# A transformer layer in split fp32 on one core: weight sums moved to VectorE, more warming products, softmax scaling issued a slot later, output weights rounded earlier, norm loads two steps ahead

## The chip, the cores and the metric

The kernel runs on one core of a Trainium2 chip. A core has five engines that work side by side, each through its own queue in order: TensorE (PE, matrix products, with a loader PEld for the stationary operand), VectorE (DVE), ScalarE (ACT), GpSimd (POOL) and SyncE (SP, which here only issues transfers). 16 DMA engines move data between HBM and the on-chip memory. Products accumulate in PSUM banks; the other operands lie in SBUF. The metric is the device time of one execution in microseconds (us); less is better. Engines wait for one another through semaphores.

## What is computed

One layer of a streaming encoder on x of 2048 tokens by 1024, all in float32:

```python
h = rms_norm(x, g_pre_mix[i])
m = chunk_relpos_attention(h, w_qkv[i], w_o[i], rel_bias[...])
x = x + rms_norm(m, g_post_mix[i])
h = rms_norm(x, g_pre_ffn[i])
x = x + rms_norm(swiglu(h, w_gate[i], w_up[i], w_down[i]), g_post_ffn[i])

def chunk_relpos_attention(h, w_qkv, w_o, rel_bias):
    q, k, v = split_heads(h, w_qkv)               # 16 heads of 64
    for c in range(n_chunks):                     # chunks of 64 frames
        ...                                       # keys: the chunk and the 8 before it
        sc = einsum('bhqd,bhkd->bhqk', q_blk, k[:, :, k0:k1]) * scale + bias
        p = softmax(sc)
        outs.append(einsum('bhqk,bhkd->bhqd', p, v[:, :, k0:k1]))
    return merge_heads(concatenate(outs)) @ w_o

def swiglu(h, w_gate, w_up, w_down):              # inner width 2816
    return (silu(h @ w_gate) * (h @ w_up)) @ w_down
```

## The kernel before

**Products.** Each float32 operand is split into a rounded high part and the rest: ACT copies it to the fast float32 format (`hi`), DVE subtracts that from the original (`lo`). `split_part` (L131, L132) does it for weights, `split` (L341, L342) for activations. A product is then three matmuls, high by high, high by low and low by high (`products`, L185 to L187), so in the profile each product shows as L185, L186 and L187.

**Seven block products.** The projections (V, then Q and K), gate/up and down are computed in 2 by 2 blocks with seven products and not eight, in the order B11, B21, T1, T2, B22, T3, T4 of activation blocks; each has a weight factor, A11, A12, S1, S2, S4, S3 or A22. S1 to S4 are sums or differences of weight blocks A. The tokens are worked in two groups of 1024 (g = 0, 1). In group 0, `block_items` loads the A blocks, and `sum_` (L834) makes the sums in place, on POOL, and stores each to HBM by a transfer from POOL's queue (L835); in group 1, `stored_items` loads them back. There are 68 sums: 8 for V, 16 for Q/K (4 chunks of columns), 44 for gate/up (11 chunks). A weight goes through a `Stream`, which loads and splits a few items ahead of PE's use; its float32 copies lie in a ring of eight tiles (`w4`, called raw in the profile), the split ones in a ring of four (`w`).

**Stages**, by their place in the span: the projections (`project`, 0 to about 505 us: V of group 0 until about 100, Q/K of group 0 until about 305, then group 1), attention (505 to 1162), the last part of the output product (to 1200), gate/up of group 0 (1200 to 1650), and the rest of the feed-forward network (to the end).

**The start.** PE first does nine products of 128 x 128 on an identity (L1256, two rows each in the profile), then V's first blocks as x arrives. The pre-norm is not applied to x but to the products: the sum of squares goes to `ms` (mean square, on DVE: L275 in the first token half, L1301 where it comes from ACT's squares by token, L1297), POOL raises it to −1/2 (`hr`, L277, L1302), and PE spreads it (`prs`, L337); `add_square` (L252, L253) collects the squares. Q and K are scaled (L420) and split (L422, L423) as they come, after DVE has added up the block products (L1224).

**Attention.** 128 slots, each two heads by 128 queries; 32 slots make a quarter of the tokens. `scores` (of slot t + 3) makes PE's scores (`st`, L493, L494), on DVE the sum with the bias and the row extreme (L502), on ACT the exponential and row sums (L506), on DVE the reciprocal (L510) and on POOL the scaling (L513). `transposed` (of slot t) turns the weights by PE (`tt`, L528; out to `pT` by DVE L531 and ACT L533), `fifth` the last block of keys (L542, L543), and `output` (after four slots) multiplies with v (L558) and splits the result (L341, L342). Between the slots, `fill` works off the output product of the quarter before (`o_quarter`, `mm` in the profile); in the first quarter there is none. `take` fetches its weights a slab ahead (`fetch`: load and split, 32 loads in all).

**Background steps.** Norm sums and residual additions (`Blocks.sums`, `Late.sums`, `Late.write`) are lists of steps, taken from the deque `later` as PE's products are issued (`tick`). `behind(w, n, lag, load, use)` lays a loop out so that the load of step k stands `lag` steps ahead of its use. Their tiles come from small rings (`scratch` of four, `io` of three).

**What sets the order.** PE's order is that of the program. On DVE, ACT, POOL and SP a scheduler sets it from the dependencies and the place in the program, so moving a statement need not move its instruction; each queue then runs in order.

Of the kernel before, what the change touches and what calls it, by code (L numbers as in the profile page):

```python
# [9 lines left out]
F32 = mybir.dt.float32  # L10
F32R = mybir.dt.float32r
I32 = mybir.dt.int32
AF = mybir.ActivationFunctionType
# [36 lines left out]
def trunk(  # L50
# [79 lines left out]
    def split_part(hi, lo, raw):  # L130
        act.activation(hi, raw, AF.Copy)  # L131
        dve.tensor_tensor(lo, raw, hi.bitcast(F32), op=ALU.subtract)  # L132

    def fetch():
        n = len(ready)
        if n == len(plan):
            return
        tiles = [w_tile(f"{n}_{c}") for c in range(2)]
        for c in range(2):
            here = slice(c * 1024, c * 1024 + 1024)  # L140
            if "fp" in phase:
                part = phase["fp"].tile([P, 1024], F32, tag="w4", name=f"raw_{n}_{c}", bufs=phase["w4"])
            else:
                part = phase["ap"].tile([P, 1024], F32, tag="raw", name=f"raw_{n}_{c}", bufs=2)
            sp.dma_start(part, plan[n][:, here])
            split_part(*tiles[c], part)
        ready.append(tiles)

# [17 lines left out]

    def take(ahead=True):

        n = taken[0]
        taken[0] += 1  # L170
        if len(ready) == n:
            fetch()
        if ahead:
            fetch()
        return Slab(ready[n])
# [256 lines left out]
    class Attend:  # L432
# [45 lines left out]
        def scores(self, ib):  # L478
# [17 lines left out]
            for h in range(2):  # L496
# [11 lines left out]
                )  # L508
                self.sc[ib, h] = sc
            dve.reciprocal(rows[:, 2:4], rows[:, 0:2])  # L510
            for h in range(2):
# [33 lines left out]
        def output(self):  # L545
# [16 lines left out]
            if p == 0:  # L562
                ats[n] = Cols(((0, 1), (2, 3))[n % 2])
            split(ats[n].hi(p), ats[n].lo(p), po)

    def o_quarter(n):
# [4 lines left out]
        for d2 in range(KT // 2):  # L571
            w = take()
            if last and d2 == KT // 2 - 1:
                back.ahead(-2)
            for dt in (2 * d2, 2 * d2 + 1):
                pt = dense_bank(dt)
                c = slice((dt % 2) * P, (dt % 2) * P + P)
                for k in range(KT):
                    products(pt, w.hi(k, c), w.lo(k, c), src.hi(k), src.lo(k), k == 0, k == KT - 1)
                    yield 3 * C512  # L580
                t = io("y")
                act.activation(t, pt, AF.Copy)
                sp.dma_start(o_d[n][:, dt, :], t)
                add_square(pt, osums[n], dt == 0)

    class Blocks:
# [8 lines left out]
        def sums(self, w, on_all=False):  # L595
# [4 lines left out]
            for t in range(2):  # L600
# [13 lines left out]

                steps += behind(w, KT, 1, load, use)
                if on_all:
# [206 lines left out]
    def block_items(src, key, early=True, ahead=None):  # L823
# [9 lines left out]
        def sum_(name, to, a, b, op=ALU.add):  # L833
            pool.tensor_tensor(r[to], r[a], r[b], op=op)  # L834
            last_pool[0] = pool.dma_start(sums_d[key][name], r[to])  # L835
# [248 lines left out]
    class Late:  # L1084
# [5 lines left out]
        def sums(self, w):  # L1090
# [10 lines left out]

            return behind(w, KT, 1, load, use)

# [11 lines left out]
        def write(self, w, eng=dve):  # L1115
# [14 lines left out]

            return behind(w, KT, 1, load, use)

# [119 lines left out]
    def project():  # L1252

        warm = ps.tile([P, HALF], F32, tag="mm", name="warm")
        for _ in range(9):
            pe.matmul(warm[:, 0:P], ident, ident, start=True, stop=True)  # L1256
# [268 lines left out]
    for t in range(AHEAD):  # L1525
        ahead(t)
    for t in range(slots):
        share = (0.4 if t % 4 == 0 else 1.2) * left[0] / max(per - t % per - 1, 1)
        if t > 0 and t % 4 == 0:
            fill(0.45 * share)  # L1530
            jobs[t // 4 - 1].output()
            if t % per == 0:
# [13 lines left out]
    jobs[-1].output()  # L1546
    fill(1e9)
# [91 lines left out]
```

## Time and profile before

| | |
|---|---|
| three runs | 2500.98, 2501.5, 2511.96 us; median 2501.5 |
| the profiled execution | 2506.22 us, of it 2504.4 from the first to the last instruction (the span) |
| mean granted clock of TensorE | 0.982 |
| HBM traffic | 529.73 MB moved by DMA, 212 GB/s on average |

The profile tells, for every instruction, its engine, line, tiles (out<-in), start and length, and what ended the idle time before it. "PE prs L337 <- POOL hr L1302" reads: PE was idle ahead of the instruction of line 337 that writes prs, until POOL's instruction of line 1302, which writes hr, was done. x and a number is how many. The granted clock is the share of TensorE's full clock that it ran at. The rows themselves stand in the prediction.

### The profile page before, as it was taken

The page shows a single profiled execution, that of the slowest core. Times are in us where ns is not written, and L with a number is a line of the kernel's source. Part 1 is how long each engine was busy: PE and PEld are TensorE (multiplying, and loading weights), DVE is VectorE, ACT ScalarE, POOL GpSimd, SP SyncE. Part 2 cuts the span into 40 slices and gives each one's busy share as a digit, 9 for nine tenths or more (in the row PEclk, how much of TensorE's full clock was granted, in tenths as well). Part 3 has the DMA queues.
Part 4 walks back from the last instruction along what each step waited for, and adds up shares of the span by engine and source line. Part 5 has one row for each costly group of instructions (what it writes and reads, how often), then busy time and mean ns, then how long its engine had stood idle before and what let it go on. Part 6 is the DMA issues. An engine that isn't in the chain of part 4 may idle for free.

```text
span 2504.4 us, 33018 instructions
## 1 busy us (share of the span) xinstructions
PE 2360.5 (94%) x11442; PEld 1914.6 (76%) x11442; DVE 1672.8 (67%) x2557; ACT 1162.8 (46%) x2039; POOL 498.2 (20%) x490
## 2 busy tenths in 40 slices
PE   7899999978888899898999999999999999999998
PEld 6677788856666677666888878888888888888887
DVE  8768856556555565566977687676657657555567
ACT  6443743346555565565532333355443333334454
POOL 4223012123332433431433233300000000000002
PEclk8999999989999999999999999999999999999999
DMA  6466789999767877784576654457765755547654
GB/s 252 161 228 215 250 240 325 298 240 258 215 169 194 244 201 204 227 230 156 185 249 222 219 180 156 151 202 226 235 237 170 249 182 190 175 146 246 193 188 153
DMA packets 229783, 529.73 MB, mean 212 GB/s; under 512 B 26320, under 2 KB 42720, under 8 KB 225136
## 3 DMA queue, kind: packets, MB, share of 16 engines
q1 hardware_dynamic: 217712, 480.42, 60.9%
q0 software_dynamic: 11904, 47.19, 6.2%
q8 instruction: 91, 1.49, 0.3%
q14 instruction: 76, 0.62, 0.1%
HBM read 380.14 MB, written 170.44 MB: 220 GB/s over the span
## 4 chain that ended last, share of the span: by engine, by line
PE 54%; DVE 2%; ACT 1%; issue 1%; DMA 0%; POOL 0%; DVEq 0%; SPq 0%; ACTq 0%
PE pd L187 6%; PE pd L185 6%; PE pd L186 6%; PE pb L186 4%; PE pb L187 4%; PE pb L185 4%; PE pc L186 3%; PE pc L187 3%; PE pc L185 3%; PE pa L185 3%; PE pa L186 3%; PE pa L187 3%; PE po L558 1%; PE mm L187 1%; PE mm L185 1%; PE mm L186 1%
## 5 line engine op out<-in xcount | busy, mean ns | idle before, releaser
L513 POOL TENSOR_SCALAR sc<-sc,rows 128x640 f32<-128x640 f32 (+4 forms) x256 | 194.7, 773 | 399.7 <-DVE rows L510 197.7
L834 POOL TENSOR_TENSOR raw<-raw,raw 128x1024 f32<-128x1024 f32 x68 | 179.9, 2646 | 394.3 <-DMA raw<-in_w_gu 139.6
L506 ACT ACTIVATE sc<-sc,rows 128x640 f32<-128x640 f32 (+4 forms) x256 | 192.9, 755 | 112.6 <-DVE rows L502 112.4
L502 DVE CUSTOM_DVE_ANT_0 sc<-st,bias 128x640 f32<-128x640 f32 (+2 forms) x248 | 176.0, 746 | 86.0 <-PE st L494 60.4
L185 PE MATMUL pb<-hb,w_wg_T 128*128 128x512 f32 x528 | 205.6, 389 | 0.0
L187 PE MATMUL pb<-hb,w_wg_T 128*128 128x512 f32 x528 | 205.4, 389 | 0.0
L186 PE MATMUL pb<-hb,w_wg_T 128*128 128x512 f32 x528 | 205.4, 389 | 0.0
L528 PE MATMUL tt<-ident,sc 128*128 128x128 f32 x928 | 140.6, 281 | 45.6 <-DVE pT L531 21.5
L277 POOL TENSOR_TENSOR rs<-ms,neg_half 128x4 f32<-128x4 f32 (+1 forms) x7 | 7.9, 1125 | 854.8 <-DVE ms L275 854.8
L528 PEld LDWEIGHTS tt<-ident,sc 128*128 128x128 f32 x928 | 105.0, 143 | 82.2 <-issue 72.1
L493 PE MATMUL st<-k,q 128*128 128x384 f32 (+3 forms) x440 | 140.7, 340 | 28.0 <-DVE rows L502 23.1
L187 PE MATMUL pd<-a,w_d_T 128*128 128x512 f32 (+1 forms) x368 | 139.8, 380 | 0.1
L185 PE MATMUL pa<-hb,w_wg_B 128*128 128x512 f32 x352 | 137.7, 391 | 2.4 <-ACT terms L922 2.4
L185 PE MATMUL pd<-a,w_d_T 128*128 128x512 f32 (+1 forms) x368 | 139.9, 380 | 0.0
L186 PE MATMUL pd<-a,w_d_T 128*128 128x512 f32 (+1 forms) x368 | 139.7, 380 | 0.0
L186 PE MATMUL pa<-hb,w_wg_B 128*128 128x512 f32 x352 | 137.7, 391 | 0.0
L187 PE MATMUL pa<-hb,w_wg_B 128*128 128x512 f32 x352 | 137.5, 391 | 0.0
L943 ACT ACTIVATE terms<-terms 128x512 f32<-128x512 f32 x65 | 41.1, 632 | 195.9 <-DVE terms L941 195.9
L494 PE MATMUL st<-k,q 128*128 128x384 f32 (+3 forms) x440 | 129.9, 315 | 0.0
L531 DVE COPY pT<-tt 128x512 f32<-128x512 f32 (+3 forms) x128 | 81.6, 637 | 69.6 <-ACT hb L341 36.2
L342 DVE TENSOR_TENSOR a<-raw_a,a 128x512 fp32r<-128x512 f32 x154 | 105.7, 694 | 30.1 <-ACT a L341 29.9
L558 PE MATMUL po<-pT,v 128*64 128x384 f32 (+3 forms) x864 | 125.2, 436 | 0.0
(265 smaller groups left out, 6343.6 us busy)
## 6 DMA issues: line engine op xcount, KB each, us to landing
raw<-in_w_gu SPq DMA_DIRECT2D x77, 512.0 KB, 4.1
q<-q SPq DMA_DIRECT2D x62, 512.0 KB, 6.7
k<-k SPq DMA_DIRECT2D x55, 512.0 KB, 9.2
s_g_S<-raw POOLq DMA_DIRECT2D x44, 512.0 KB, 3.1
raw_d<-d_S SPq DMA_DIRECT2D x88, 256.0 KB, 3.6
raw_a<-aT SPq DMA_DIRECT2D x88, 256.0 KB, 3.6
raw<-s_g_S SPq DMA_DIRECT2D x44, 512.0 KB, 3.8
bias<-ext_d SPq DMA_DIRECT2D x124, 144.0 KB, 9.2
```

What stands on the lines that cost most here:

```text
L185: pe.matmul(pt, a_hi, b_hi, start=first, stop=False, skip_group_check=go_on)
L186: pe.matmul(pt, a_hi, b_lo, start=False, stop=False, skip_group_check=go_on)
L187: pe.matmul(pt, a_lo, b_hi, start=False, stop=last, skip_group_check=go_on)
L342: eng.tensor_tensor(lo, src, hi.bitcast(F32), op=ALU.subtract)
L493: pe.matmul(st[:, a:b], q[:, 2 * h, cols], kk[:, h, key], start=True, stop=False)
L494: pe.matmul(st[:, a:b], q[:, 2 * h + 1, cols], kk[:, h, key], start=False, stop=True)
L502: dve.tensor_tensor_reduce(out=sc[:, :n], in0=st[:, c0 : c0 + n], in1=rev, scale=-1.0, scalar=3.0e38, op0=ALU.add, op1=ALU.min, accum_out= ...
L506: act.activation(sc[:, :n], sc[:, :n], AF.Exp, bias=nmax, scale=-1.0, accum_out=rows[:, h : h + 1])
L513: last_pool[0] = pool.tensor_scalar(sc[:, :n], sc[:, :n], rows[:, 2 + h : 3 + h], 1.0, op0=ALU.mult, op1=ALU.mult)
L528: pe.transpose(tt[:, u, :], sc[h][:, b * P : b * P + P], ident)
L558: pe.matmul(po[heads[h], c0:c1], v[:, kb, c : c + 64], self.pT[:, h, r, c0:c1], start=m == 0, stop=m == len(terms) - 1,)
L834: pool.tensor_tensor(r[to], r[a], r[b], op=op)
```

## The change

Five parts:

1. `sum_` adds on DVE and no longer on POOL; the store remains on POOL's queue.
2. 28 warming products, not 9.
3. `scores` ends after the exponentials; the reciprocal and the scaling are a new method `scaled`, called in the next slot, between `transposed` and the new scores. `output` only rounds the high part and returns a function for the low part, which runs after the new scores.
4. Output weights: `fetch` only loads a slab, `part_split` splits half of it, in the middle and near the end of every second output tile of the slab ahead. The first slab is loaded at slot 16 and split at slots 20 and 22.
5. `behind` has lag 2 in `Blocks.sums`, `Late.sums` and `Late.write`.

```diff
+    raws = []
     def fetch():
-        n = len(ready)
+        n = len(raws)
...
             sp.dma_start(part, plan[n][:, here])
-            split_part(*tiles[c], part)
-        ready.append(tiles)
+            parts.append(part)
+        raws.append(parts)
+
+    def part_split(c):
+        n = len(ready) - (c > 0)
+        if n == len(raws):
+            return
+        if c == 0:
+            ready.append([w_tile(f"{n}_{i}") for i in range(2)])
+        split_part(*ready[n][c], raws[n][c])
...
-    def take(ahead=True):
+    def take():
...
+        if len(raws) == n:
+            fetch()
         if len(ready) == n:
-            fetch()
-        if ahead:
-            fetch()
+            part_split(0)
+            part_split(1)
+        fetch()
...
+            self.open = (ib, rows, n)
+
+        def scaled(self):
+            ib, rows, n = self.open
             dve.reciprocal(rows[:, 2:4], rows[:, 0:2])
...
-            split(ats[n].hi(p), ats[n].lo(p), po)
+            act.activation(ats[n].hi(p), po, AF.Copy)
+            return lambda: dve.tensor_tensor(ats[n].lo(p), po, ats[n].hi(p).bitcast(F32), op=ALU.subtract)
...
                     yield 3 * C512
+                    if k == 3 and len(ready) == taken[0] and dt % 2:
+                        part_split(0)
+                    elif k == KT - 2 and dt % 2 and len(ready) > taken[0]:
+                        part_split(1)
...
-                steps += behind(w, KT, 1, load, use)
+                steps += behind(w, KT, 2, load, use)
...
         def sum_(name, to, a, b, op=ALU.add):
-            pool.tensor_tensor(r[to], r[a], r[b], op=op)
+            dve.tensor_tensor(r[to], r[a], r[b], op=op)
             last_pool[0] = pool.dma_start(sums_d[key][name], r[to])
...
-        for _ in range(9):
+        for _ in range(28):
             pe.matmul(warm[:, 0:P], ident, ident, start=True, stop=True)
...
     for t in range(AHEAD):
         ahead(t)
+        if t < AHEAD - 1:
+            jobs[0].scaled()
...
-            jobs[t // 4 - 1].output()
+            low = jobs[t // 4 - 1].output()
...
+        if t == 16:
+            fetch()
+        elif t in (20, 22):
+            part_split(t // 2 - 10)
         job = jobs[t // 4]
         job.transposed(t % 4)
+        if t + AHEAD - 1 < slots:
+            jobs[(t + AHEAD - 1) // 4].scaled()
         ahead(t + AHEAD)
+        if t > 0 and t % 4 == 0:
+            low()
```

How the scheduler lays the queues out, in three places. The new program's line numbers are higher: L253 is L265 there, L342 is L354, L675 is L697, L275 is L287, the sum's L834 is L856, L1297 is L1319, L510 is L527, L502 is L514, L531 is L548.

DVE at the start, before (w_wv are V's weights, hb the blocks of x, total the sum of squares):

```order
10 L132 TENSOR_TENSOR w_wv_B_330<-raw_283,w_wv_B_330 128x1024
11 L132 TENSOR_TENSOR w_wv_B_339<-raw_285,w_wv_B_339 128x1024
12 L253 TENSOR_TENSOR total<-total,sq 128x512 x2
13 L342 TENSOR_TENSOR hb_4_357<-hb_2_287,hb_4_357 128x512 x2
14 L253 TENSOR_TENSOR total<-total,sq 128x512 x2
15 L342 TENSOR_TENSOR hb_4_357<-hb_2_287,hb_4_357 128x512 x2
16 L675 TENSOR_TENSOR hb_1_276<-hb_1_276 128x512
17 L275 TENSOR_SCALAR ms<-pssq 128x4
18 L132 TENSOR_TENSOR w_wv_T_434<-raw_289,w_wv_T_434 128x1024
```

DVE at the same place now (two rows more of total, hb_4 and sums stand ahead of these, like them):

```order
18 L265 TENSOR_TENSOR total<-total,sq 128x512
19 L354 TENSOR_TENSOR hb_4_376<-hb_2_306,hb_4_376 128x512
20 L265 TENSOR_TENSOR total<-total,sq 128x512
21 L856 TENSOR_TENSOR raw_313<-raw_313,raw_315 128x1024
22 L354 TENSOR_TENSOR hb_4_376<-hb_2_306,hb_4_376 128x512
23 L856 TENSOR_TENSOR raw_300<-raw_300,raw_313 128x1024
24 L697 TENSOR_TENSOR hb_1_295<-hb_1_295 128x512
25 L856 TENSOR_TENSOR raw_304<-raw_304,raw_300 128x1024
26 L354 TENSOR_TENSOR hb_5_443<-hb_1_295,hb_5_443 128x512
27 L132 TENSOR_TENSOR w_wv_T_453<-raw_308,w_wv_T_453 128x1024
28 L132 TENSOR_TENSOR w_wv_T_456<-raw_313,w_wv_T_456 128x1024
29 L287 TENSOR_SCALAR ms<-pssq 128x4
```

The root's `ms` stood right behind the subtractions of hb_4 and stands now behind six sums (L856), the first subtraction of hb_5 and two weight roundings; the sums alternate with the subtractions that PE waits for.

ACT, the squares by token (L1297, of `terms` tiles that SP fills) in the V stage, before:

```order
58 L1297 ACTIVATE terms,ssq<-terms 128x1024
59 L341 ACTIVATE hb_6_554<-hb_1_276 128x512
60 L1169 ACTIVATE terms<-pv 128x512
61 L131 ACTIVATE w_wv_B_625<-raw_283 128x1024
62 L131 ACTIVATE w_wv_B_628<-raw_285 128x1024
63 L695 ACTIVATE t_800<-hb_1_276 128x512
64 L1297 ACTIVATE terms,ssq<-terms 128x1024
65 L695 ACTIVATE t_801<-hb_1_276 128x512
66 L695 ACTIVATE t_802<-hb_1_276 128x512
67 L695 ACTIVATE t_803<-hb_1_276 128x512
68 L341 ACTIVATE hb_8_741<-hb_1_276 128x512 x3
69 L1297 ACTIVATE terms,ssq<-terms 128x1024
```

and now:

```order
48 L1319 ACTIVATE terms,ssq<-terms 128x1024
49 L1191 ACTIVATE terms<-pv 128x512
50 L717 ACTIVATE t_819<-hb_1_295 128x512
51 L1191 ACTIVATE terms<-pv 128x512
52 L353 ACTIVATE hb_6_573<-hb_1_295 128x512
53 L717 ACTIVATE t_820<-hb_1_295 128x512
54 L353 ACTIVATE hb_6_573<-hb_1_295 128x512
55 L1319 ACTIVATE terms,ssq<-terms 128x1024
```

The last of the four squarings, which the second root needs, stood ahead of row 70 and stands ahead of row 56; the two weight roundings w_wv_B, which stood ahead of it, stand behind it.

DVE in an attention slot, before and now, where the reciprocal of a slot is written a slot later in the program:

```order
813 L531 COPY pT<-tt 128x4x128 [waits PE_49]
814 L510 RECIPROCAL rows<-rows 128x2 [waits Activation_49]
815 L502 ISA sc,rows<-st,bias_4109 128x640 [waits DMAHW0_49,DMAHW7_49,PE_49,Pool_49]
816 L502 ISA rows 128x1
817 L502 ISA sc,rows<-st,bias_4114 128x640 [waits DMAHW2_49,DMAHW1_49]
```

```order
835 L548 COPY pT<-tt 128x4x128 [waits PE_49]
836 L527 RECIPROCAL rows<-rows 128x2 [waits Activation_49]
837 L514 ISA sc,rows<-st,bias_4125 128x640 [waits DMAHW0_49,DMAHW7_49,PE_49,Pool_49]
838 L514 ISA rows 128x1
839 L514 ISA sc,rows<-st,bias_4130 128x640 [waits DMAHW2_49,DMAHW1_49]
```

The reciprocal stands where it stood, behind the copy of the turned weights and ahead of the next slot's scores, and waits for the same engine; so it is in nearly all slots.

More of the change, by code (lines that the diff above doesn't have):

```diff
@@ L132, in split_part @@
         dve.tensor_tensor(lo, raw, hi.bitcast(F32), op=ALU.subtract)
+    raws = []
     def fetch():
-        n = len(ready)
+        n = len(raws)
         if n == len(plan):
             return
-        tiles = [w_tile(f"{n}_{c}") for c in range(2)]
+        parts = []
         for c in range(2):
@@ L1100, in use @@
                 add_square(c.pop(dt), self.total, dt == 0)
-            return behind(w, KT, 1, load, use)
+            return behind(w, KT, 2, load, use)
         def rstd(self, wait):
@@ L1129, in use @@
                 sp.dma_start(self.dst[:, dt, :], y)
-            return behind(w, KT, 1, load, use)
+            return behind(w, KT, 2, load, use)
     rs, rows_of = [], {}
@@ L1540, in trunk @@
                     later.extend(blocks[0].sums(2.0))
+        if t == 16:
+            fetch()
+        elif t in (20, 22):
+            part_split(t // 2 - 10)
         job = jobs[t // 4]
         job.transposed(t % 4)
+        if t + AHEAD - 1 < slots:
+            jobs[(t + AHEAD - 1) // 4].scaled()
         ahead(t + AHEAD)
+        if t > 0 and t % 4 == 0:
+            low()
         fill((0.55 if t % 4 == 0 else 1.0) * share)
         job.fifth()
-    jobs[-1].output()
+    jobs[-1].output()()
     fill(1e9)
```

## The prediction

> **What bounds the kernel now.** I read the page's totals first, then TensorE's waits, then busy time by stretch, then timelines around each long wait.
>
> ```profile
> PE 2360.5 (94%) x11442; PEld 1914.6 (76%) x11442; DVE 1672.8 (67%) x2557; ACT 1162.8 (46%) x2039; POOL 498.2 (20%) x490
> ...
> PE st L493 <- DVE rows L502: 29.9, 34, 5.2
> PE pb L185 <- DVE terms L1224: 13.1, 5, 4.0
> PE prs L337 <- POOL hr L1302: 9.6, 1, 9.6
> PE mm L185 <- ACT w L131: 6.9, 2, 3.7
> PE tt L528 <- DVE rows L510: 6.3, 6, 1.1
> PE pv L187 <- DVE hb L342: 5.6, 5, 2.3
> ```
>
> TensorE (PE) works 2360.5 of 2504.4 us, so the whole idle time that any edit can win back is 144 us, plus what a cold clock costs. The change adds no product but small warming ones, so it must earn its gain from the waits above (us in total, times, longest).
>
> ```profile
> 0.00:50.00 50.00, 37.45 (x131) 28.56 (x131) 40.02 (x31) 29.36 (x46) 27.26 (x23) 0.83 0.66 262
> 50.00:100.00 50.00, 39.55 (x157) 31.18 (x158) 40.03 (x58) 32.65 (x52) 4.01 (x3) 0.86 0.41 138
> 305.00:495.00 190.00, 190.00 (x840) 157.36 (x839) 115.97 (x153) 77.02 (x105) 34.80 (x48) 1.00 0.94 287
> 1200.00:1250.00 50.00, 50.00 (x225) 41.50 (x224) 46.66 (x51) 28.63 (x45) 21.91 (x13) 1.00 0.50 176
> 1300.00:1650.00 350.00, 344.81 (x1517) 284.42 (x1516) 256.07 (x290) 118.30 (x161) 104.02 (x65) 1.00 0.53 181
> ```
>
> The columns are length, busy time of PE, its loader, VectorE (DVE), ScalarE (ACT) and GpSimd (POOL), granted clock, DMA share. PE idles 12.6 and 10.5 us in the first two stretches and runs at 0.83 and 0.86 of its clock; from 305 to 495 it never idles (840 products in 190 us, 0.226 us each); in the first token group of gate/up (1200 to 1650) it idles next to nothing in the first 50 us and 5.2 in the last 350. So gains are to be had at the start, in the Q/K products behind it and in attention, and hardly in the feed-forward part, where 44 of the 68 moved sums lie.
>
> **Part 1, the sums on DVE.** A sum costs POOL 2646 ns, and it stretches what DVE does beside it.
>
> ```profile
> L834 POOL TENSOR_TENSOR raw<-raw,raw 128x1024 f32<-128x1024 f32 x68 | 179.9, 2646 | 394.3 <-DMA raw<-in_w_gu 139.6 <-DVE w_wg_B L132 91.2 <-DVE w_wq_B L132 53.7
> ...
> 14.69 1.29 DVE L342 TENSOR_TENSOR hb<-hb,hb 128x512 fp32r<-128x512 f32 x2
> 18.44 6.44 DVE L253 TENSOR_TENSOR total<-total,sq 128x512 f32<-128x512 f32 x2
> 24.80 6.65 DVE L342 TENSOR_TENSOR hb<-hb,hb 128x512 fp32r<-128x512 f32 x2
> 34.64 1.22 DVE L132 TENSOR_TENSOR w_wv_T<-raw,w_wv_T 128x1024 fp32r<-128x1024 f32 x1
> 37.80 8.35 DVE L132 TENSOR_TENSOR w_wv_T<-raw,w_wv_T 128x1024 fp32r<-128x1024 f32 x1
> ```
>
> Alone, two half-width (512) operations take 1.29 us, 0.65 each, and a 1024-wide one 1.22; beside POOL's sums the same forms take 6.44, 6.65 and 8.35. In these three rows DVE loses 5.2 + 5.4 + 7.1 = 17.7 us. A sum on DVE isn't in the trace; its bounds are the 1024-wide subtraction (1.22) and POOL's 2.65. I take 1.22, the same engine and shape: 8 sums at the start cost 9.8 us and give back 17.7.
>
> Now the path. PE there waits for two roots of norms, whose rows are these, in order of time:
>
> ```profile
> 34.80 1.96 POOL L277 TENSOR_TENSOR hr<-ms,neg_half 128x4 f32<-128x4 f32 x1 [3.92 <-DVE ms L275]
> 38.23 1.05 PE L337 MATMUL prs<-ident,hr 128*128 128x128 f32 x4
> 50.20 0.64 PE L187 MATMUL pv<-w_wv_T,hb 128*128 128x512 f32 x1 [1.82 <-DVE hb L342]
> 74.09 1.06 ACT L1297 ACTIVATE terms<-terms 128x1024 f32<-128x1024 f32 x1 [1.39 <-DMA terms<-in_xt]
> 75.53 1.04 POOL L1302 TENSOR_TENSOR hr<-ms,neg_half 128x4 f32<-128x4 f32 x1 [25.55 <-DVE ms L1301]
> 76.63 1.11 PE L337 MATMUL prs<-ident,hr 128*128 128x128 f32 x4 [9.63 <-POOL hr L1302]
> ```
>
> *First root.* In the new order ms stands behind 6 sums, 9 half-width operations and 2 weight roundings: from 18.4, that is 8 x 1.22 + 9 x 0.65 = 15.6 us, so ms at 34.0 to 34.3, just ahead of the root as before (34.80). The root, 1.96, ends at 36.3 and prs starts at 36.5 instead of 38.23, where PE still had products to do: −1.7. But PE, whose operands now come without stretch (its waits for hb were up to 2.3 us), is done by about 30 and stands there idle: the waits for hb are replaced by one for the root of some 6 us. *This is what is late next.*
>
> *Second root.* PE's second prs was ready at 67.0 (76.63 less its wait of 9.63), 28.8 us after the first, with 1.82 us of that in the gap before 50.20 and, behind it, some 8 products at half clock (0.2 us each too much, 1.6; the pitch is worked out in part 2). Without these it is ready at 36.5 + 28.8 − 3.4 = 61.9. Its release: ACT squares the tokens in four pieces, the last at 74.09; in the new order these stand some 14 rows earlier, as do their loads. DVE ahead of that ms has 26 half-width rows and 6 wide ones, 16.9 + 7.3 = 24.2 us, from 34.3: not before 58.5. With some 4 us of waits for PE's and ACT's results I take ms at 62.6 and, 1.5 us on, prs at 64.1, against 76.63: **−12.5**. Bounds: −14.7 (PE ready, 61.9), and −2 (the last squaring stays where it was, only the first root's gain is left).
>
> *Q/K.* These rows stand just ahead of the waits for L1224:
>
> ```profile
> 145.88 2.40 DVE L420 TENSOR_TENSOR terms<-terms,row 128x512 f32<-128x512 f32 x1
> 148.97 2.72 DVE L423 SCALAR_TENSOR_TENSOR lo<-terms,hi 128x512 fp32r<-128x512 f32 x1 [0.70 <-ACT hi L422]
> 155.51 0.47 PE L185 MATMUL pb<-hb,w_wq_T 128*128 128x512 f32 x1 [3.99 <-DVE terms L1224]
> 195.22 2.84 DVE L423 SCALAR_TENSOR_TENSOR lo<-terms,hi 128x512 fp32r<-128x512 f32 x1
> 198.70 2.77 DVE L420 TENSOR_TENSOR terms<-terms,row 128x512 f32<-128x512 f32 x1
> 198.81 0.47 PE L185 MATMUL pb<-hb,w_wq_T 128*128 128x512 f32 x1 [2.91 <-DVE terms L1224]
> ```
>
> At 146 to 151, DVE loses 1.75 + 2.1 = 3.8 us by the half-width price, and PE waits 3.99; at 195 to 201 it loses 2.2 + 2.1 = 4.3, and PE waits 2.91 and then again. One or two sums now stand in the same queue, 1.2 to 2.4 us each time. So 1.4 to 3.1 us come back each time, **−4** for both. The rest of the 13.1 us has no sum beside it. Bounds: 0 to −8.1 (no sum in the way).
>
> *Gate/up.* 44 sums add 44 x 1.22 = 54 us to DVE. What comes back:
>
> ```profile
> L952 DVE TENSOR_TENSOR T<-terms,T 128x512 f32<-128x512 f32 x43 | 51.4, 1196 | 0.1
> L952 DVE TENSOR_TENSOR T<-b,terms 128x512 f32<-128x512 f32 x22 | 15.1, 686 | 0.1
> ...
> POOL raw L834 <- DMA raw<-in_w_gu: 139.6, 9, 32.6
> ```
>
> 43 x (1196 − 686) = 22 us in one group; at the start of the program a sum cost DVE more than it will itself, here the other groups were stretched less. DVE's load grows by nothing to 32 us in 450, and what PE waits there, 5.2 us, is all that can be won: **−2**, bounds −5.2 and +14 (second rival). POOL waited nine times for the weights themselves; DVE will now wait there in its place, with the evacuations of PE's banks queued behind it.
>
> **Part 2, warming.** 19 more products add 38 rows to 18. At the row's own 0.234 us they end at 14.4, past the first product:
>
> ```profile
> 1.35 4.21 PE L1256 MATMUL warm<-ident 128*128 128x128 f32 x18 [1.35 <-POOL ident masks.py:199]
> 10.22 0.80 PE L185 MATMUL pv<-w_wv_B,hb 128*128 128x512 f32 x1 [4.66 <-ACT hb L341]
> 18.30 0.63 PE L187 MATMUL pv<-w_wv_B,hb 128*128 128x512 f32 x1
> 18.72 0.63 PE L185 MATMUL pv<-w_wv_B,hb 128*128 128x512 f32 x1
> ```
>
> From start to start a product takes 0.42 us here, and 0.226 at full clock (840 in 190 us, above). If the clock came up only late, this part would cost 14.4 − 10.2 = 4.2 us; if it were up at 10.2, the 8.5 us until 18.72 would shrink by up to a half, 4. Both vanish in PE's new wait of some 6 us for the first root, which they end before: 0, with −4 to +4 only where that wait isn't there. [...]
>
> **Part 3, reciprocals and scaling a slot later.** In DVE's new order the reciprocals stand, in almost every slot, where they stood: the scheduler had put them there already. POOL's scalings and the low halves likewise. I cost it 0; the wait that it is about is 6.3 us on PE, and it could also cost as much.
>
> **Part 4, output weights.**
>
> ```profile
> 630.44 0.61 PE L185 MATMUL mm<-hb,w 128*128 128x512 f32 x1 [3.73 <-ACT w L131]
> 629.35 1.99 ACT L131 ACTIVATE w<-raw 128x1024 fp32r<-128x1024 f32 x2
> ```
>
> At the end of the first quarter PE waits 3.73 us while ACT rounds the first slab (1.99) behind its exponentials, then 9 products run at half clock: 3.7 + 9 x 0.2 = 5.5. The slab is now rounded in the slots 20 and 22, where DVE's rows hold PE up (29.9 us in all) and two subtractions can add at most 2 x 1.22 = 2.4. I take **−4**; bounds −5.5 and +2.4. Later slabs move half a slab, between attention rows of the same number: 0.
>
> **Part 5, norms two steps ahead.** Their tiles come from a ring of four that is full already; SP's loads keep their places. 0, bounds ±3.
>
> **Sum.** −12.5 − 4 − 2 − 4 = −22.5, from the profiled execution's 2506.2 (span 2504.4): 2483.7. That execution stands 4.7 above the median, 2501.5, of the runs shown; measured from there, **2479**.
>
> **Rivals.** *The second root stays late.* ms stands behind DVE's whole queue; if waits in that queue, which now hold also for the loads of the weights, push it to 73, the start gives 2 and not 12.5: −12, 2490. For it: DVE was busy 40 us of each 50 there; against: 17.7 of that was stretch. Chance 0.2, a quarter of it beyond the 0.5% line.
>
> *DVE blocks on weights (slower).* At each of 11 chunks the first sum stands in DVE's queue within some microseconds of its load's landing, POOL waited 139.6 us in nine such places, and DVE works 46.7 of the first 50 us. Where the wait exceeds the slack of 3 to 11 us that DVE has in the 41 of a chunk (3.3 of 50, 94 of 350), PE's banks aren't emptied. At 3 us a chunk beyond the slack: 33 − 20 = +13, 2515. It decides from about 2 us a chunk (22 against 20). Chance 0.05: POOL took its waits when it had nothing else to do, and mostly long before the sum was due.
>
> *Stores starve (slower).* Each of 17 S3 sums overwrites a tile that a POOL-queue store still reads, so DVE now waits for that landing.
>
> ```profile
> s_g_S<-raw POOLq DMA_DIRECT2D x44, 512.0 KB, 3.1
> ```
>
> At 3.1 us each, all exposed, 53 − 22 = +31, 2532. The order puts S3 ten and more rows behind that store: chance 0.02. [...]
>
> *It does more.* Part 3 takes effect or PE is ready at both roots: −33, 2468; chance 0.08.
>
> **Chances.** Forecast 0.65, the rest as above. A measurement tells 0.5%, 12.5 us: bounds 2489.0 and 2514.0. Faster: 0.65 less a tail of 0.05, + 0.08 + 0.05 from the late root = 0.73; same 0.21; slower 0.06. The range runs from 2464 (most of the bounds of the good side) to 2504 (late root, and other terms at nothing).
>
> **What would show it.** Right: no DVE row over 2.5 us for one or two operations before 105 us; ms of the second root near 62, PE's wait before prs twice, about 6 and 3 us; no 3.7 us wait at the first output product; DVE 46 of 50 us in gate/up as before. Wrong: DVE rows in gate/up that wait for DMA raw, with PE idle over 10 us between 1200 and 1650; or reciprocals whose wait for sc has gone.

## The result and the profile after

| | before | changed |
|---|---|---|
| median | 2503.36 us (2500.98 to 2511.96, 4 runs) | 2479.15 us (2478.01 to 2480.74, 4 runs) |
| ratio | | 0.9898, 95% interval 0.9872 to 0.9923 |
| span of the profiled execution | 2504.4 us | 2477.4 us |

The change takes 24.2 us off the median, 27.0 off the profiled span. A later set of runs of the same changed kernel has 2476.3 (2475.2 to 2477.8) beside 2504.1 before, 0.9889 (0.9876 to 0.9902).

From the page of the changed kernel, the busy times, and then TensorE's waits (us in total, times, longest):

```profile
PE 2356.4 (95%) x11480; PEld 1916.3 (77%) x11480; DVE 1651.3 (67%) x2625; ACT 1163.5 (47%) x2039; POOL 313.6 (13%) x422
...
PE st L505 <- DVE rows L514: 26.8, 29, 5.2
PE tt L545 <- DVE pT L548: 25.2, 25, 1.9
PE tt L545 <- ACT pT L560: 13.7, 24, 1.3
PE st L505 <- DMA k<-k: 9.1, 3, 4.1
PE tt L545 <- DVE rows L527: 5.0, 5, 1.1
PE prs L349 <- POOL hr L289: 4.6, 1, 4.6
PE pb L197 <- DVE terms L1246: 4.5, 3, 3.5
PE mm L197 <- ACT w L131: 3.2, 1, 3.2
```

The wait for the second root (9.6 us) has left this list and one for the first root (4.6) stands in its place; the wait ahead of the Q/K sums fell from 13.1 to 4.5; that for k's transfer rose from 4.4 to 9.1, and that for the turned weights (tt <- DVE pT) from 21.5 to 25.2. DVE is busy 21 us less, though it has taken over 68 sums.

Stretches of the same limits as before (length, then PE, PEld, DVE, ACT, POOL, clock, DMA share):

```profile
0.00:50.00 50.00, 40.72 (x187) 33.60 (x188) 38.03 (x51) 41.60 (x67) 6.30 (x15) 0.93 0.82 312
50.00:100.00 50.00, 48.11 (x213) 39.14 (x212) 43.37 (x62) 25.79 (x39) 2.71 (x5) 1.00 0.48 163
...
1200.00:1250.00 50.00, 50.00 (x228) 41.60 (x227) 43.78 (x59) 21.83 (x30) 3.66 (x6) 1.00 0.61 214
...
1300.00:1650.00 350.00, 346.86 (x1527) 285.97 (x1526) 260.44 (x338) 126.96 (x178) 16.01 (x30) 1.00 0.54 189
```

The second stretch had 39.55 us of PE at 0.86 of the clock and has 48.11 at 1.00. In gate/up DVE's load hardly moves (46.66 to 43.78, 256 to 260): 44 more operations, and the longer rows beside POOL's sums (the stretch) gone.

The timelines of the start, DVE and then PE:

```profile
18.73 1.48 DVE L265 TENSOR_TENSOR total<-total,sq 128x512 f32<-128x512 f32 x2
20.13 1.22 DVE L856 TENSOR_TENSOR raw<-raw,raw 128x1024 f32<-128x1024 f32 x1
...
31.76 2.35 DVE L132 TENSOR_TENSOR w_wv_T<-raw,w_wv_T 128x1024 fp32r<-128x1024 f32 x2
34.03 0.15 DVE L287 TENSOR_SCALAR ms<-pssq 128x4 f32<-128x4 f32 x1
...
61.05 0.16 DVE L1323 TENSOR_SCALAR ms<-ssq 128x4 f32<-128x4 f32 x1
```

```profile
35.37 1.11 PE L349 MATMUL prs<-ident,hr 128*128 128x128 f32 x4 [4.63 <-POOL hr L289]
...
62.38 0.65 PE L349 MATMUL prs<-ident,hr 128*128 128x128 f32 x4 [1.27 <-POOL hr L1324]
```

A sum takes 1.22 us on DVE, and no row beside it is stretched (the two additions that took 6.44 take 1.48). The two roots' means stand at 34.0 and 61.1, and PE waits for them 4.6 and 1.3 us.

**Where the time went.** PE's order is the same in all kernels here but for the warming products, so the same product can be found in each trace. The table is worked out from the traces: the start of a product in a kernel less its start in the kernel before, in us. Its last row is a product near the end.

| start before | what stands there | changed | sums_only | v_on_pool | gu_on_pool | sums_on_pool | lag1 | parts_134 |
|---|---|---|---|---|---|---|---|---|
| 76.6 | second prs | −14.3 | −16.4 | +1.2 | −16.2 | −3.9 | −14.1 | −16.2 |
| 105 | end of V, group 0 | −16.4 | −18.5 | +0.6 | −18.4 | −3.7 | −16.3 | −18.4 |
| 300 | Q/K of group 0 done | −25.7 | −29.0 | −10.3 | −28.2 | −3.9 | −27.6 | −30.0 |
| 524 | first attention slots | −25.7 | −29.1 | −10.3 | −28.2 | −3.8 | −27.9 | −30.0 |
| 665 | first output products | −26.7 | −30.1 | −9.6 | −27.3 | −5.3 | −32.6 | −35.9 |
| 850 | half of attention | −27.0 | −30.4 | −9.9 | −27.7 | −5.6 | −32.9 | −36.2 |
| 1190 | last output products | −23.0 | −30.2 | −11.6 | −27.4 | −0.2 | −34.2 | −38.1 |
| 1345 | gate/up, third chunk | −24.9 | −32.1 | −13.5 | −24.7 | −0.2 | −36.2 | −40.1 |
| 1380 | behind it | −22.3 | −32.0 | −13.4 | −24.7 | +5.0 | −36.1 | −40.0 |
| 1650 | gate/up of group 0 done | −26.7 | −36.3 | −17.7 | −26.5 | +3.0 | −40.4 | −44.3 |
| 2450 | near the end | −26.7 | −35.7 | −17.4 | −25.6 | +3.0 | −38.5 | −44.4 |

The changed kernel wins 16.4 in V and 9.3 in Q/K, then little in the first quarter of attention, gives 4 back in the later ones and wins 3.7 in gate/up. One trace differs from the next of the same kernel: after_again, the changed kernel once more, stands at −15.2, −29.1, −30.8, −26.1, −24.2 and −28.4 at 76.6, 300, 665, 1190, 1380 and 2450.

### The profile page after: what moved, and what is told of

Its sections match the earlier page's. It is cut to its first block, busy times and chain, and to the rows that moved or that the text cites. A ratio compares the mean times of both kernels' runs of the same rounds, so it can differ in the third digit from the quotient of the medians.

```text
span 2477.4 us, 33015 instructions
## 1 busy us (share of the span) xinstructions
PE 2356.4 (95%) x11480; PEld 1916.3 (77%) x11480; DVE 1651.3 (67%) x2625; ACT 1163.5 (47%) x2039; POOL 313.6 (13%) x422
## 4 chain that ended last, share of the span: by engine, by line
PE 54%; DVE 2%; issue 1%; ACT 1%; DMA 1%; POOL 0%; DVEq 0%; SPq 0%; POOLq 0%; ACTq 0%
PE pd L199 6%; PE pd L197 6%; PE pd L198 6%; PE pb L197 5%; PE pb L199 5%; PE pb L198 5%; PE pa L199 3%; PE pa L198 3%; PE pa L197 3%; PE pc L199 3%; PE pc L198 3%; PE pc L197 3%; PE po L575 1%; PE mm L199 1%; PE mm L197 1%
## 5 line engine op out<-in xcount | busy, mean ns | idle before, releaser
L514 DVE CUSTOM_DVE_ANT_0 sc<-st,bias 128x640 f32<-128x640 f32 (+2 forms) x248 | 176.1, 745 | 95.8 <-PE st L506 66.1
L545 PE MATMUL tt<-ident,sc 128*128 128x128 f32 x928 | 144.1, 286 | 46.1 <-DVE pT L548 25.2
L548 DVE COPY pT<-tt 128x512 f32<-128x512 f32 (+3 forms) x128 | 81.5, 637 | 66.6 <-PE tt L545 34.5
L131 ACT ACTIVATE w_wg_T<-raw 128x1024 fp32r<-128x1024 f32 x88 | 92.9, 1057 | 70.1 <-PE pa L199 30.8
L354 DVE TENSOR_TENSOR a<-raw_a,a 128x512 fp32r<-128x512 f32 x154 | 105.7, 694 | 28.8 <-ACT a L353 28.3
L575 PE MATMUL po<-pT,v 128*64 128x256 f32 (+3 forms) x864 | 124.6, 436 | 0.0
```

The source lines that it names most:

```text
L354: eng.tensor_tensor(lo, src, hi.bitcast(F32), op=ALU.subtract)
L514: dve.tensor_tensor_reduce(out=sc[:, :n], in0=st[:, c0 : c0 + n], in1=rev, scale=-1.0, scalar=3.0e38, op0=ALU.add, op1=ALU.min, accum_out= ...
L545: pe.transpose(tt[:, u, :], sc[h][:, b * P : b * P + P], ident)
L575: pe.matmul(po[heads[h], c0:c1], v[:, kb, c : c + 64], self.pT[:, h, r, c0:c1], start=m == 0, stop=m == len(terms) - 1,)
```

## The experiments

| kernel | what it is | median us (range) | ratio to before, 95% interval |
|---|---|---|---|
| sums_only | before + part 1 | 2469.6 (2468.6 to 2471.1) | 0.9862 (0.9849 to 0.9874) |
| sums_on_pool | changed − part 1 | 2507.7 (2497.7 to 2513.0) | 1.0013 (1.0002 to 1.0025) |
| v_on_pool | sums_only, V's 8 on POOL | 2488.9 (2482.3 to 2491.4) | 0.9930 (0.9916 to 0.9944) |
| gu_on_pool | sums_only, gate/up's 44 on POOL | 2474.9 (2471.1 to 2480.7) | 0.9879 (0.9862 to 0.9896) |
| warm9 | changed − part 2 | 2472.5 (2471.4 to 2478.4) | 0.9879 (0.9864 to 0.9894) |
| sums_warm | before + parts 1, 2 | 2472.7 (2470.9 to 2475.1) | 0.9869 (0.9855 to 0.9882) |
| scaled_as_before | changed − part 3 | 2480.8 (2477.7 to 2484.9) | 0.9907 (0.9894 to 0.9919) |
| weights_as_before | changed − part 4 | 2481.3 (2478.5 to 2486.1) | 0.9910 (0.9897 to 0.9924) |
| sums_weights_late | before + parts 1, 4, first slab 8 slots later | 2467.3 (2465.2 to 2468.8) | 0.9851 (0.9838 to 0.9864) |
| lag1 | changed − part 5 | 2467.4 (2465.7 to 2468.3) | 0.9852 (0.9839 to 0.9865) |
| after_again | changed | 2476.3 (2475.2 to 2477.8) | 0.9889 (0.9876 to 0.9902) |
| parts_134 | before + parts 1, 3, 4 | 2461.9 (2460.9 to 2469.8) | 0.9833 (0.9818 to 0.9848) |

The kernels after the first result were run in three sets, each with the kernel before beside it: sums_only, sums_on_pool, warm9 and weights_as_before; then after_again, lag1, scaled_as_before and sums_weights_late; then the other four. The changed kernel was 2.9 us faster in after_again than in the first result, with ranges that don't touch, and faster than the 2478 to 2482 expected of it, while the kernel before was 0.7 slower. So a difference of some 3 us between kernels of different sets doesn't stand by itself.

### The sums: sums_only and sums_on_pool

```diff
-            pool.tensor_tensor(r[to], r[a], r[b], op=op)
+            dve.tensor_tensor(r[to], r[a], r[b], op=op)
```

in the kernel before, and the reverse in the changed one.

> The kernel before with part 1 alone: the 68 sums on VectorE, nothing else. Theory A (the stretch of VectorE beside GpSimd's sums is nearly all of the gain): the second prs at 62 to 65 us (76.6 before, 62.4 in the changed kernel), Q/K of group 0 another 8 to 11 us, the end at 2478 to 2486. Rival B (the gain is spread over the five parts, the sums give the start alone): 2487 to 2493.

> The changed kernel with the sums back on GpSimd, the other four parts kept. Theory A: all but 5 us of the gain is gone, 2497 to 2505, with the second prs near 75. Rival B: 2488 to 2494.

Part 1 alone takes 34.8 us off (2504.4 to 2469.6), more than the whole change and more than either theory gave it; without it nothing is gained (2507.7, above both theories too). So theory A holds in its direction, and it put part 1 too low: the other four parts, taken together, **cost** some 7 to 10 us. The wait that the prediction took for the danger, DVE on weights still on their way, is small. From the groups of sums_only:

```profile
L834 DVE TENSOR_TENSOR raw<-raw,raw 128x1024 f32<-128x1024 f32 x68 | 82.9, 1219 | 5.8 <-DMA raw<-in_w_gu 2.4 <-DMA res<-in_x 2.3 <-issue 0.7
...
L952 DVE TENSOR_TENSOR T<-terms,T 128x512 f32<-128x512 f32 x43 | 29.4, 684 | 0.1
```

POOL waited 139.6 us for these loads, DVE 2.4 (0.8 in the changed kernel). And 43 rows of T, 1196 ns each before, are back at 684.

### Which sums: v_on_pool and gu_on_pool

Both are sums_only with one line more, which gives V's sums (8) or gate/up's (44) back to GpSimd:

```diff
-            dve.tensor_tensor(r[to], r[a], r[b], op=op)
+            (pool if key.startswith("v") else dve).tensor_tensor(r[to], r[a], r[b], op=op)
```

> Part 1 alone (2469.6), but V's 8 sums back on GpSimd; 60 stay on VectorE. Theory A (the start's 18.5 us are V's sums and the clock behind the waits that they make): the second prs at 74 to 77 us, 2485 to 2490. Rival J (the start's gain comes from the new order of ScalarE's squares, which any move of sums brings): the second prs at 62 to 68, 2472 to 2480.

> Part 1 alone (2469.6), but gate/up's 44 sums back on GpSimd. By the landmarks of the trace these 44 brought 5.2 us between 1200 and 1560. Theory A: 2473 to 2476, PE idle 5 to 9 us between 1200 and 1650 (1.7 with part 1 alone, 6.3 before). Rival K (VectorE blocks on weights there, so that GpSimd is the better place for these 44): 2463 to 2468.

V's 8 sums are worth 19 of the 35 us (2488.9 against 2469.6). In v_on_pool the stretched rows and the wait for the second root are those of before:

```profile
18.19 6.43 DVE L253 TENSOR_TENSOR total<-total,sq 128x512 f32<-128x512 f32 x2
24.54 6.64 DVE L342 TENSOR_TENSOR hb<-hb,hb 128x512 fp32r<-128x512 f32 x2
...
37.92 8.21 DVE L132 TENSOR_TENSOR w_wv_T<-raw,w_wv_T 128x1024 fp32r<-128x1024 f32 x1
...
77.80 1.11 PE L337 MATMUL prs<-ident,hr 128*128 128x128 f32 x4 [10.70 <-POOL hr L1302]
```

So rival J falls as it was put: moving the other 60 sums doesn't bring the squares forward. ACT's last squaring starts at 74.28 there, as in the kernel before (74.09), and at 49.33 in sums_only. But with V's sums the stretch of DVE and the old order of the squares (and of their loads on SP) come back together, so these runs don't show how much of the second root's gain is the stretch and how much the new order; that stays open. Q/K still wins its 10.9 there (+0.6 to −10.3 in the table). Gate/up's 44 sums are worth some 5 us (2474.9 against 2469.6, with intervals that overlap a little; by landmarks the stretch from 1190 to 1650 wins 6.2 with them on DVE and loses 0.9 with them on POOL). In gu_on_pool PE waits again for the roots on POOL, and T is stretched again:

```profile
PE prs L337 <- POOL rs L277: 5.3, 3, 2.3
...
L952 DVE TENSOR_TENSOR T<-terms,T 128x512 f32<-128x512 f32 x43 | 51.8, 1205 | 0.1
```

### Warming: warm9 and sums_warm

`range(28)` back to `range(9)` in the changed kernel; `range(9)` to `range(28)` in sums_only.

> The changed kernel with 9 warming products. Theory A (as the prediction has it, PE waits for the first root whatever it did before): the wait ahead of the first prs shrinks from 4.6 us by what the cold clock costs, the first prs stays at 35 to 36, the end at 2478 to 2481. Rival C (the clock that 28 products bring up is worth its time): the first prs 2 to 5 us later and the end at 2482 to 2485.

> Parts 1 and 2: the sums on VectorE and 28 warming products, against 2469.6 for the sums alone. Theory L (28 products change the scheduler's order so that two weight roundings stand ahead of the second root's ms, which is 6 us later, and PE waits there): the second prs 1.5 to 2.5 us later than with the sums alone (60.2), the end at 2471 to 2474. The prediction's step (no effect): 2469 to 2470.5. Rival M (the warming itself helps): 2465 to 2468.

Both say that 28 products cost 3 us or more: 2472.5 against 2476.3 to 2479.2, and 2472.7 against 2469.6, the first with ranges that touch, the second from two sets. lag1 and parts_134, further below, differ in part 2 alone and are a third pair: 2467.4 with 28 products and 2461.9 with 9, five runs of which one (2469.8) is above lag1's. None of warm9's expectations was right: the first prs came at 35.6, as theory A said, but the end is below both. The clock did come up: the first of the windows below counts 18 warming rows and the second, which is shorter, 29. (The column of the clock reads 1.00 in both; there the count of rows tells them apart.) From the windows of the changed kernel at its start, and of before:

```profile
1.00:5.00 4.00, 3.65 (x18) 3.65 (x19) 0.00 (x0) 1.03 (x2) 0.29 (x1) 1.00 0.68 194
5.00:8.00 3.00, 3.00 (x29) 3.00 (x29) 1.74 (x2) 2.74 (x5) 0.00 (x0) 1.00 0.99 309
...
10.00:15.00 5.00, 1.71 (x4) 0.64 (x4) 3.13 (x5) 4.41 (x8) 0.00 (x0) 0.99 1.02 423
15.00:20.00 5.00, 4.99 (x15) 3.97 (x16) 4.72 (x6) 5.00 (x8) 0.00 (x0) 0.67 1.01 422
```

```profile
10.00:15.00 5.00, 3.95 (x7) 1.86 (x8) 4.12 (x6) 4.87 (x9) 0.00 (x0) 0.50 1.01 422
15.00:20.00 5.00, 5.00 (x13) 3.86 (x14) 4.83 (x5) 5.00 (x9) 2.10 (x1) 0.53 1.02 425
```

From 10 to 15 the clock is 0.99 and not 0.50, but PE works 1.7 of the 5 us: it waits for hb, whose 4 products come when ACT and DVE have made them, and by 15 to 20 the clock is at 0.67 again. One price of the products is elsewhere. They change where the scheduler puts other rows: DVE and PE at the second root, sums_only first, then sums_warm:

```profile
55.03 0.16 DVE L1301 TENSOR_SCALAR ms<-ssq 128x4 f32<-128x4 f32 x1
...
56.31 1.22 DVE L132 TENSOR_TENSOR w_wv_B<-raw,w_wv_B 128x1024 fp32r<-128x1024 f32 x1
...
60.22 0.65 PE L337 MATMUL prs<-ident,hr 128*128 128x128 f32 x4 [0.40 <-POOL hr L1302]
```

```profile
56.70 1.23 DVE L132 TENSOR_TENSOR w_wv_B<-raw,w_wv_B 128x1024 fp32r<-128x1024 f32 x1 [1.10 <-ACT w_wv_B L131]
...
58.65 1.23 DVE L132 TENSOR_TENSOR w_wv_B<-raw,w_wv_B 128x1024 fp32r<-128x1024 f32 x1
...
60.39 0.16 DVE L1301 TENSOR_SCALAR ms<-ssq 128x4 f32<-128x4 f32 x1
...
61.73 0.65 PE L337 MATMUL prs<-ident,hr 128*128 128x128 f32 x4 [1.25 <-POOL hr L1302]
```

With 28 products ms stands behind two weight roundings that wait for ACT, 5.4 us later, and PE's prs is 1.5 us later. The other two pairs show the same: ms at 55.2 in warm9 and in parts_134, at 61.1 in the changed kernel and 61.2 in lag1, and prs some 2 us apart. So theory L holds for 1.5 to 2 us. Where the rest arises isn't shown: the two traces here end only 0.5 us apart (−35.2 and −35.7 at 2450).

### Scaling: scaled_as_before

The change's `scaled` joined to `scores` again, and the low part to `split`.

> The changed kernel with reciprocals and scaling written as before (part 3 undone). Its queues differ from the changed kernel's in 34 rows of VectorE and none of ScalarE and GpSimd. The prediction's step (the scheduler had done it already): 2478 to 2481, and the loss at 985 to 1130 stays. Rival G (those few rows are the loss at 985 to 1130): 2474 to 2477.

2480.8, not faster than the changed kernel (2476.3 beside it, 2479.2 in the first runs), so rival G falls and part 3 costs nothing. Whether it saves up to 4 us isn't settled: of the 5.7 us between the traces of scaled_as_before and of the first result 3.6 arise ahead of attention, at a wait of Q/K's products in group 1 (415 us in its trace), where part 3 has no row.

### Output weights: weights_as_before and sums_weights_late

The first is the changed kernel with `fetch` and `take` of before; the second is sums_only with part 4, and

```diff
-        if t == 16:
+        if t == 24:
             fetch()
-        elif t in (20, 22):
-            part_split(t // 2 - 10)
+        elif t in (28, 30):
+            part_split(t // 2 - 14)
```

> The changed kernel with the output weights fetched and rounded as before (part 4 undone). In the trace of the changed kernel PE loses 7.1 us between 579 and 592 (by the clock of before) and wins 7.3 back at 627 to 646. Theory A (the loss is that the first slab's 1 MB is loaded at slot 16 ahead of q and k on the one queue, the gain is that it is rounded early): both go, q and k land as before, and the end is at 2478 to 2481. Rival D (the loss is a chance delay of transfers): the loss stays, the 3.7 us wait at the first output product comes back, the end is at 2484 to 2488.

> Parts 1 and 4 alone, with the first slab of output weights loaded at slot 24 and rounded at 28 and 30 (slots 16, 20 and 22 in the change). Theory A of part 4 (its early load pushes q and k back by the transfer time of 1 MB and costs 7 us, its early rounding saves 6 to 7): later, where slots hold more work and the queue has caught up, it costs at most 2 and saves the same 5 to 7: 2463 to 2468. Rival H (the load costs the same wherever it stands in this quarter): 2469 to 2472.

Two rows of the changed kernel, then one of weights_as_before:

```profile
553.81 0.30 PE L505 MATMUL st<-k,q 128*128 128x128 f32 x1 [2.07 <-DMA k<-k]
...
568.00 0.45 PE L505 MATMUL st<-k,q 128*128 128x128 f32 x1 [2.94 <-DMA k<-k]
```

```profile
600.91 0.79 PE L185 MATMUL mm<-hb,w 128*128 128x512 f32 x1 [3.73 <-ACT w L131]
```

Without part 4 the first two waits go and the third comes back, so both effects are the part's own, as theory A has it: loading the slab at slot 16 puts 1 MB ahead of q and k. SP issues the two loads at 547.38; the q and k issued from 545 to 570 land in 12.1 and 12.5 us (medians), and in 6.5 and 7.2 in the same stretch of weights_as_before. In the changed kernel's trace the part costs 7 us by landmarks from 575 to 600 (clock of before) and saves 7 from 615 to 660; over seven traces with part 4 as written the balance from 524 to 665 lies between −1 and −6, over five without it between −1 and +1.6. As a whole part 4 saves some 2 to 5 us by medians (2481.3, just above theory A's 2478 to 2481, against 2476.3 to 2479.2), with ranges that touch those of the first result. Eight slots later PE still waits for k (1.7 and 1.9 us), so theory A's "at most 2" failed, and 2467.3 is in A's range; against 2469.6, of another set, it is a gain of 2.3.

### Norm loads: lag1

```diff
-                steps += behind(w, KT, 2, load, use)
+                steps += behind(w, KT, 1, load, use)
```

and the same in `Late.sums` and `Late.write`.

> The changed kernel with the norm loads one step ahead (part 5 undone). With the sums alone the kernel took 2469.6, 9.5 less than the changed one, so parts 2 to 5 together cost that much. Theory E (part 5 moves VectorE's and SP's rows from the second attention half on and costs its share: about 4 us at 985 to 1130 and 2.6 to 4 at 1345 to 1380): 2471 to 2475. Rival F (part 5 does nothing, as the prediction had it; those losses come from part 3 or 4): 2477 to 2481.

2467.4 beside 2476.3: part 5 costs 9 us, all of theory E and more. warm9 and parts_134 differ in it alone too (2472.5 and 2461.9). The landmarks have it in two places, and they part all traces: the six with lag 2 lose 2 to 7 us from 850 to 1190 and 2.6 to 5.2 from 1345 to 1380, the seven with lag 1 at most 0.6 and 0.1. The first place is attention's third and fourth quarter (+4.0 in the changed kernel, −1.4 in lag1). There, in the changed kernel, DVE, PE and the issue of one load:

```profile
986.87 0.69 DVE L548 COPY pT<-tt 128x512 f32<-128x512 f32 x1
990.40 0.75 DVE L1147 SCALAR_TENSOR_TENSOR y<-y,gt,osum 128x512 f32<-128x512 f32 x1 [2.84 <-issue]
991.06 0.16 DVE L527 RECIPROCAL rows<-rows 128x2 f32<-128x2 f32 x1
...
992.61 0.69 DVE L548 COPY pT<-tt 128x512 f32<-128x512 f32 x1
...
993.45 0.63 PE L545 MATMUL tt<-ident,sc 128*128 128x128 f32 x4 [1.92 <-DVE pT L548]
...
985.17 0.38 SPq L72 DMA_DIRECT2D y<-o  x1
...
y<-o SPq DMA_DIRECT2D x1, 256.0 KB, 5.1
```

The load of y was issued at 985.17 and landed 5.1 us later, at 990.3; the row that uses it starts at 990.40. Behind it on DVE stand a reciprocal, two rows of scores and the copy pT that PE waits for. "issue" in the bracket means no releaser was found; the landing names it. With lag 1 this use stands 15 rows later on DVE, two slots on, and its load 13 places later on SP (issued at 998.85; the use waits 0.63 us). So lag 2 moves the load forward as well, but only to the place ahead of one slot's q, k and bias, behind the store of an older tile (x<-y, 984.75), and the use to where its transfer has just begun. Why the load comes no earlier is only argued: its tiles are from rings of unchanged size, so it can be issued when an older one is stored, whatever the lag. From this wait to 999 the changed kernel falls 2.5 us further behind lag1, of 5.3 in this place; the rest is spread over several later waits. The second place is gate/up's third chunk. ACT and PE of the changed kernel, and ACT of lag1:

```profile
1337.70 0.63 ACT L260 ACTIVATE row<-sum 128x512 f32<-128x512 f32 x1 [6.98 <-DMA sum<-x]
1338.24 1.04 ACT L131 ACTIVATE w_wg_B<-raw 128x1024 fp32r<-128x1024 f32 x1
...
1347.76 0.47 PE L197 MATMUL pb<-hb,w_wg_T 128*128 128x512 f32 x1 [2.30 <-DVE terms L963]
```

```profile
1323.40 1.06 ACT L131 ACTIVATE w_wg_B<-raw 128x1024 fp32r<-128x1024 f32 x1 [3.94 <-issue]
```

ACT waits 7 us for a load of the next norm (issued at 1331.58), with the weight rounding behind it, then DVE's rounding and sums, and PE. In lag1 the rounding stands ahead of the row that waits for that load: lag 2 moved this row 7 places forward on ACT, the load 3 on SP.

### The best version: parts_134

The changed kernel with `range(9)` and lag 1.

> The changed kernel without its parts 2 and 5: 9 warming products, lag 1. Theory (parts 2 and 5 cost 2 to 4 and 9, part 4 saves 0 to 3): 2463 to 2467, faster than the changed kernel and than the sums alone. Rival: the three together bring nothing beyond the sums, 2468 to 2471.

2461.9 us, 0.9833 (0.9818 to 0.9848), under the expected 2463: faster than the changed kernel by 14 to 17 us. Parts 3 and 4 beside part 1 bring 7.7 more than part 1 alone (2469.6, of another set).

## Why the prediction was right, and where its steps were wrong

The time was forecast as 2479 and measured as 2479.15. The sum is right because errors cancel: part 1 was worth 34.8 us and not 18.5, and parts 2 and 5, both put at nothing, cost 3 or more and 9. That the time came within 0.2 us is luck once more: the gain was 24.2 and not 22.5, and the kernel before stood 1.9 us higher beside this run (2503.4) than the 2501.5 that the forecast started from. By steps, with the changed kernel's landmarks:

- **First root**, forecast prs 36.5 with a new wait of some 6 us: 35.4 and 4.6. Right, and it is what was late next. The root itself took 1.04 us and not 1.96. In the kernel before it starts 0.16 us behind a DVE row of 1.22 us (34.64); whether that row made it longer isn't shown.
- **Second root**, forecast −12.5, ms at 62.6, prs at 64.1: −14.3, 61.1, 62.4. Right in what it named, less stretch and earlier squares; v_on_pool shows that V's 8 sums make both, not how much is due to each. PE's wait there is 1.3 us, where about 3 was named. What the sum left out is the clock *behind* the wait: from prs to the end of V another 2.1 us are won, since PE, which waits 1.3 us here and not 9.6, goes on at full clock (1.00 from 63 to 67, 0.50 from 77 to 81 in the kernel before). The prediction had counted such a term for the gap at 50.20 alone.
- **Q/K**, forecast −4: −9.3, and 10.5 with the sums alone. This term was mis-sized twice. The sums do stand in the queue ahead of the first wait as forecast (two of 1.22 us, at 128.75 and 133.42), and yet it shrinks from 3.99 to 0.82: DVE's run of rows up to it begins 1.9 us earlier by the landmarks, its idle time for ACT's rounding of w_wq_B being 0.73 and not 2.65 us. The second (2.91) is gone. And the products at half clock behind the first wait weren't counted (0.50 from 157 to 159 in the kernel before; behind the second it is 1.00 from 198.8 to 201): around 156 the landmark moves by 3.2 at the wait and 1.6 more behind it.
- **Gate/up**, forecast −2: −3.7, and −6.2 with the sums alone. The bound of −5.2 was idle time without the clock (0.91 from 1500 to 1520 in the kernel before, 1.00 in the changed one), and without the 1.1 us that PE idles from 1250 to 1300. DVE's load didn't grow by "nothing to 32 us"; it fell a little (343.4 to 340.1 us from 1200 to 1650, from windows of the same limits).
- **Part 2**, forecast 0 from both sides: +3 or more. The reason given (PE waits for the first root anyway) held; what failed is that only PE's time was priced. The rows that the scheduler moves in answer to 19 more products weren't looked at. The 0.234 us a row, by which the 56 rows were to end at 14.4, is the mean of the kernel before with the last row's end; from start to start its rows take 0.213 us behind the first (0.38), and none is faster than the others. But that says nothing of the rows behind the 18th: in the changed kernel they follow one another in 0.11 us, and the 56 rows end at 9.4 us and not at 14.4.
- **Part 3**, forecast 0: not faster when undone. Right, so far as it can be told.
- **Part 4**, forecast −4: −1 in the first trace, −2 to −5 by medians. Its price had DVE's subtractions in it and not the 1 MB that SP loads: the DMA of a moved step, in the quarter whose transfers PE already waited for.
- **Part 5**, forecast 0 with bounds ±3: +9. The step that failed: "SP's loads keep their places". They don't: in the two places above load and use both move forward, by 13 places and 15 rows, and by 3 places and 7 rows. The *uses* weren't looked at. A use that comes earlier on DVE or ACT than its load has landed is a wait at the head of an in-order queue (2.84 us at 990.40 on DVE, 6.98 at 1337.70 on ACT).
- **Rivals.** DVE blocking on gate/up's weights: 2.4 us in sums_only, 0.8 in the changed kernel. Stores that DVE waits for: by the groups above no sum waited for one (of 5.8 us of waits in sums_only, 4.7 are for two loads and 0.7 are issue). The late root: didn't happen. More than forecast (2468): not in this kernel; sums_only (2469.6) and parts_134 (2461.9) come near it or below, by part 1's size and without parts 2 and 5, not by the condition named.

## What to carry to other kernels

When an operation moves off an engine, look for its price in the rows of the *other* engine that it made longer (T, 1196 ns with POOL's sums and 684 without), look at what the scheduler moves in answer, and add the half-clock products that the trace has behind a TensorE wait that goes (the clock is 0.50 behind the waits of 9.6 and 4.0 us in the kernel before, and 1.00 behind that of 2.9). A prefetch made deeper on paper can do harm, as here where its buffers didn't grow with it: the use moved forward in an in-order queue at least as far as the load did. A set of edits that wins can hold losers; here each of the five was worth a run of its own, and two of them had to go.

## What the runs showed of the hardware

In the trace of before, the stretch goes with who starts first, DVE's row or POOL's sum. Rows of both around two sums:

```profile
1288.18 0.68 DVE L952 TENSOR_TENSOR T<-b,terms 128x512 f32<-128x512 f32 x1
1295.14 2.88 DVE L952 TENSOR_TENSOR T<-terms,T 128x512 f32<-128x512 f32 x1
...
1288.36 2.77 POOL L834 TENSOR_TENSOR raw<-raw,raw 128x1024 f32<-128x1024 f32 x1 [1.86 <-DVE w_wg_B L132]
1294.71 2.76 POOL L834 TENSOR_TENSOR raw<-raw,raw 128x1024 f32<-128x1024 f32 x1 [2.60 <-DVE w_wg_T L132]
```

The first DVE row starts 0.18 us ahead of POOL's and takes its usual 0.68; the second starts 0.43 behind it and takes 2.88, until 0.55 us after POOL's end (1297.47). So it is in all 10 overlaps of each kind: T<-b,terms first, 0.69 at most; T<-terms,T second, 2.87 at least. Rows of DVE with one operand from PSUM aren't stretched here: the 19 of terms<-pb,terms that start beside a running sum take 0.69 at most.

The pace of the warming products rose, but not after a fixed time. Start to start they take 0.21 us at first and 0.11 later (the 56 rows take 8.1 us in the changed kernel and 8.5 in lag1); the change comes 3.3 us after the first start in the changed kernel, 6.2 in after_again, 3.0 in sums_only and 3.8 in sums_warm. In the kernel before, in warm9 and in parts_134 all 18 rows, 3.8 us from the first start to the last, keep the slow pace.
